# Layer 0's latents by feature blocks, weights stationary, from a transposed input

## Chip, cores and metric

One core of one Trainium2 chip. The metric is the device time of one execution of the whole program in microseconds (us), as the median of the runs shown. The program has two layers; the change lies in the first stage of layer 0.

## The reference, cut to what matters

SEQ = 2048 latent tokens and 256 context tokens run through two layers of width 1024. Layer 0 first modulates its input and projects it; the first 1056 columns are the latents of the attention heads:

```python
m = silu(cond) @ ada_w + ada_b                 # shift, scale, gate; one vector for x, one for the context
h = rms_norm(x, norm_g) * (1 + scale) + shift  # 2304 tokens x 1024
u = h @ w_in                                   # of it here: q_lat 768, kv_lat 256, k_rope 32
q  = (rms_norm(q_lat, q_norm) @ w_uq).reshape(n, 8, 96)
kv = (rms_norm(kv_lat, kv_norm) @ w_ukv).reshape(n, 8, 64 + 64)
k  = concat([kv[..., :64], broadcast(k_rope)])
q, k = rms_norm(q, q_gain), rms_norm(k, k_gain)
# the last 32 columns of q and k of the latent tokens are rotated (axial rope); v = kv[..., 64:]
```

The remaining columns of `u`, the attention itself, gated linear attention and layer 1 follow; they are not touched.

## The kernel before

Everything is f32. A large product is made of three products of rounded parts (`mm3`, lines 120 to 122: high by high, high by low, low by high), with each operand split into a high part `h` and a low part `l` by a pass of ScalarE (ACT) and one of VectorE (DVE). The three products are the only large work of TensorE (PE) in this stage.

`even_latent` works tile by tile: 18 tiles of 128 tokens (`NT`), the first two of them context. `prep` of a tile loads it as rows (`x`), sums its squares, scales it, turns it by eight transposes on PE (line 339, tile `px`), applies the modulation on ACT, splits it into `hhi` and `hlo`, and stores it to the scratch tensor `H`, from which later stages `reload` it. `gemm` then makes 3 x 8 x 3 products per tile with the token tile as the stationary side and 352 columns of `w_lat` (`W0`, `W1`, `W2`) as the moving side, so that a token's latents lie along a row (`u`). `scaled` takes the two root mean squares along that row and scales it. One step later `up` turns the tile again, eight transposes on PE (line 500, tile `tp`), splits it (`lth`, `ltl`), and makes the products with `w_uq` (`WU`, 36 of 384 columns) and `w_ukv` (`wkv`, 12 of 512 columns), followed by the norms and the rotation. One step later still `fin` turns q and k per head (16 transposes, line 554), splits four heads at a time into `qkhl` (two buffers) and stores them by DMAs on SP to `QA`, `QC`, `KA`, `KC`, in pieces of 512 bytes. So three tiles are in work at a time, and one tile's products stand among another's transposes and norms.

Beside that, `ada_first` makes the first modulation vectors from 8 MB of weights at the very start, and `ada_steps` makes the other eight rows of modulation in small steps: 64 loads `adaw` of 256 KB through two buffers, two DVE passes (`adac`) each, two products per row. `first` makes some of the next stage's products for the last two tiles, whose parts are kept, and `ahead` splits the next stage's weights (`w_rest`).

The order on each engine is laid down at build time: the framework places the recorded instructions by a timeline of its own and `issue_after` holds some back. Each engine, and SP and ACT as issuers of DMAs, then goes through its list in order. A DMA on SP or ACT takes one of eight semaphores in turn and waits until the DMA that had it before has landed.

`even_rest` follows: the remaining columns of `u`, woven with products (`mx`, line 660) for the maxima of the attention scores. These read `KA`, `KC`, `QA`, `QC` of all tiles back (`mk`, `mq`).

Of the kernel before, what the change touches and what calls it, by code (L numbers as in the profile page):

```python
# [88 lines left out]
class Kern:  # L89
# [151 lines left out]
    def ada_first(self, sp, pp, tags):  # L241
# [9 lines left out]
        for n, b in enumerate((0, 2, 1, 3)):  # L251
            ps = self.tl(pp, [P, 512], tags[0], bufs=2)
            for hf in range(2):
                w = self.tl(sp, [P, 4, 512], "adaw", bufs=8)
# [6 lines left out]
            pt = self.tl(pp, [P, 512], tags[1], bufs=2)  # L261
# [12 lines left out]
    def ada_steps(self, jobs, sp, pp, tag):  # L274

        nc = self.nc
        for l, b in jobs:
            acc = [self.tl(sp, [P, 512], f"adac{c}", bufs=1) for c in range(2)]
            for k in range(KD):
                w = self.tl(sp, [P, 512], "adaw", bufs=2)  # L280
# [120 lines left out]
    def even_latent(self, ws, wrest, kept):  # L401
# [6 lines left out]
        with ExitStack() as es:  # L408
            pp = self.pool(es, "epA", bufs=2, space=PSUM, reuse_waits="tile")
            px = ("px", 2)  # L410
            hT, lat, nat, win = {}, {}, {}, {}
            with ExitStack() as es2:
                st = self.pool(es2, "adaS", side="left", reuse_waits="tile")
                rows = self.transposed(0, self.i["xin"], pp, px, st)
                self.ada_first(st, pp, ("gm", "up"))
                hT[0] = self.modulate(0, 0, *rows)
                hi, lo = win[0] = [self.tl(ws, [P, KD, LAT_CHUNK], "W0" + z, F32R, bufs=1) for z in "hl"]
                for k in range(0, KD, 4):
                    w = self.tl(st, [P, 4, 512], "adaw", bufs=8)
                    nc.sync.dma_start(w[:, :, :LAT_CHUNK], self.i["w_lat"][:, 0, k : k + 4])  # L420
                    for n in range(0, 4, 2):
                        q = slice(k + n, k + n + 2)
                        self.act(hi[:, q, :], w[:, n : n + 2, :LAT_CHUNK])
                        nc.vector.tensor_tensor(out=lo[:, q, :], in0=w[:, n : n + 2, :LAT_CHUNK], in1=hi[:, q, :], op=ALU.subtract)
            wp = self.pool(es, "ewA", side="left", reuse_waits="tile")
            sp = self.pool(es, "esA", bufs=2, side="left", reuse_waits="tile")
            hT[1] = self.prep(0, 1, self.i["xin"], pp, px)
            for j in (1, 2):
                win[j] = self.split_w(ws, self.i["w_lat"][:, j], KD, LAT_CHUNK, f"W{j}", 2)
            behind = self.wload  # L430
            vec = self.tl(wp, [P, 8], "lnorm")
            nc.sync.dma_start(vec[:], self.i["lat_norm"])
            qkg = self.tl(wp, [P, 4], "qkg")
# [3 lines left out]
            wuq = self.split_w(ws, self.i["w_uq"], 6, 768, "WU", 1, rows=vec[:, 0:6])  # L437
            wkv = self.split_w(wp, self.i["w_ukv"], 2, 1024, "wkv", 1, rows=vec[:, 6:8])
# [4 lines left out]

            def gemm(*ts):
                us = {}
                for j in range(3):
                    for t in ts:
                        hi, lo = hT[t]
                        ps = self.tl(pp, [P, LAT_CHUNK], "gm", bufs=2)
                        wh, wl = win[j]  # L450
                        self.mm3(ps[:], (lambda k: hi[:, k, :], lambda k: lo[:, k, :]),
                                 (lambda k: wh[:, k, :], lambda k: wl[:, k, :]), range(KD))
                        if j == 0:
                            us[t] = self.tl(sp, [P, LAT_COLS], "u", bufs=2)
                        self.act(us[t][:, j * LAT_CHUNK : (j + 1) * LAT_CHUNK], ps[:])
                for t in ts:
                    parts = hT.pop(t)
                    if t >= NT - self.hbufs:
                        kept[t] = parts
                    scaled(t, us[t])  # L460

            def scaled(t, u):
                ss = self.tl(sp, [P, 4], "ssl")
                sq = self.tl(sp, [P, 512], "sql", bufs=1)
                self.act(sq[:, :512], u[:, :512], AF.Square, accum_out=ss[:, 0:1])
                self.act(sq[:, :256], u[:, 512:768], AF.Square, accum_out=ss[:, 3:4])
                nc.gpsimd.tensor_tensor(out=ss[:, 0:1], in0=ss[:, 0:1], in1=ss[:, 3:4], op=ALU.add)
                self.act(sq[:, :256], u[:, 768:1024], AF.Square, accum_out=ss[:, 1:2])
                self.act(sq[:, :32], u[:, 1024:], AF.Square, accum_out=ss[:, 2:3])
                self.rpow(ss[:, 0:1], ss[:, 0:1], 1.0 / Q_LORA, EPS)  # L470
                self.rpow(ss[:, 1:2], ss[:, 1:2], 1.0 / KV_LORA, EPS)
                nc.vector.tensor_scalar(out=u[:, :768], in0=u[:, :768], scalar1=ss[:, 0:1], scalar2=None, op0=ALU.mult)
# [105 lines left out]
            for s in range(NT + 2):  # L578
# [1362 lines left out]
```

## Time and profile before

| | us |
|---|---|
| runs | 3565.96, 3571.14, 3572.35 (median 3571.14) |
| profiled execution | 3570.04 |
| its span, first to last instruction | 3568.3 |
| PE busy | 3472.6 (97%) |
| DVE, ACT, POOL busy | 2341.2, 1389.5, 1275.0 |
| latent products on PE, first one | 35.17 |
| first product `mx` of the next stage | 564.88 |
| 0 to 570: PE busy, mean granted clock, DMA share | 527.92, 0.96, 0.60 |

How to read the rows quoted below: a row of a stretch has its length and then the busy time of PE, PE's weight loads, DVE, ACT and POOL with the number of instructions, PE's granted clock as a share of full speed, the DMA engines' mean busy share and GB/s. A row of the timeline has its start, its time, the engine, the line of the kernel, the operation, output and inputs, the shapes, and in brackets how long the engine stood idle before it and what ended that. A row of the chain of waits has a start, a time and what the chain passed through. A row of a group ends in its busy time, the mean of one in ns, and the idle time before it.

### The profile page before, as it was taken

The numbers are of one execution on the slowest core, as the hardware profiler recorded it, in microseconds if no ns is written. First come the engines' busy times: TensorE is split into PE (matmuls) and PEld (weight loads), VectorE is DVE, ScalarE is ACT, GpSimd is POOL, SyncE is SP. The second block draws the span as 40 slices with busy tenths as digits, with TensorE's granted clock in tenths as the row PEclk, the third lists the DMA queues.
The fourth block names the chain that finished last, engine by engine and source line by source line (L and its number), as shares of the span: only waits on it lengthen the run. The fifth ranks groups of instructions, "written<-read, shape, count | busy, mean of one in ns | idle before, by whom it ended". The sixth has DMA issues, their size and how long they took to land.

```text
span 3568.3 us, 53989 instructions
## 1 busy us (share of the span) xinstructions
PE 3472.6 (97%) x19604; PEld 2686.9 (75%) x19604; DVE 2341.2 (66%) x4624; ACT 1389.5 (39%) x2516; POOL 1275.0 (36%) x1411
## 2 busy tenths in 40 slices
PE   8999998999999999999999999999899999999899
PEld 6888987888896666665557878888688887555577
DVE  4677655888885777768874345455588784666732
ACT  5454552111113544546663124444322223555510
POOL 1333430100101333322212234333344443888763
PEclk9999999999999999999999999999999999999999
DMA  7555554222215242434526544445744447888672
GB/s 254 149 154 165 143 146 137 71 86 76 87 51 153 72 131 71 121 106 141 161 88 193 166 146 136 136 144 168 227 152 125 142 122 200 227 213 223 187 230 95
DMA packets 375868, 517.07 MB, mean 145 GB/s; under 512 B 34009, under 2 KB 253609, under 8 KB 369698
## 3 DMA queue, kind: packets, MB, share of 16 engines
q1 hardware_dynamic: 330914, 422.62, 41.3%
q0 software_dynamic: 22032, 63.00, 5.8%
q10 hardware_dynamic: 22656, 27.99, 2.2%
q8 instruction: 156, 2.56, 0.3%
q14 instruction: 110, 0.90, 0.1%
HBM read 334.17 MB, written 179.30 MB: 144 GB/s over the span
## 4 chain that ended last, share of the span: by engine, by line
PE 82%; DMA 6%; DVE 5%; ACT 2%; POOL 2%; issue 2%; SPq 1%; DVEq 0%; ACTq 0%; POOLq 0%
PE gm L129 10%; PE gm L130 10%; PE gm L131 10%; PE st L1130 9%; PE av L1040 7%; PE mx L660 4%; PE st L1587 2%; PE o L1621 2%; DMA wraw<-w_od 2%; PE pj L130 2%; PE pj L129 2%; PE pj L131 2%; PE st L131 2%; PE st L129 2%; PE st L130 2%
## 5 line engine op out<-in xcount | busy, mean ns | idle before, releaser
L661 DVE TENSOR_REDUCE mm<-mx 128x1 f32<-128x512 f32 (+1 forms) x656 | 388.4, 627 | 82.4 <-PE mx L660 75.3
L106 ACT ACTIVATE apt<-st 128x1024 f32<-128x1024 f32 (+1 forms) x296 | 300.3, 1015 | 304.9 <-PE st L1130 290.4
L1137 DVE TENSOR_TENSOR acc<-acc,apt 128x1024 f32<-128x1024 f32 x256 | 340.8, 1331 | 79.8 <-ACT apt L106 60.9
L1130 PE MATMUL st<-aq,akh 64*128 64x512 f32 x1728 | 312.0, 408 | 1.2 <-ACT apt L106 0.8
L1040 PE MATMUL av<-apt,av 128*64 128x512 f32 x1152 | 265.8, 598 | 0.0
L660 PE MATMUL mx<-mk,mq 96*128 96x512 f32 (+1 forms) x656 | 235.9, 373 | 1.0 <-DMA mq<-QC 0.6
L1746 DVE TENSOR_TENSOR opt<-st,tab 128x64 f32<-128x64 f32 (+10 forms) x576 | 144.2, 314 | 140.1 <-PE st L1588 63.9
L1627 POOL TENSOR_TENSOR oacc<-oacc,opt 128x576 f32<-128x576 f32 (+5 forms) x192 | 221.8, 1178 | 39.2 <-ACT rl L106 19.6
L1130 PE MATMUL st<-aq,akl 64*128 64x512 f32 (+1 forms) x1152 | 230.5, 390 | 0.0
L1130 PEld LDWEIGHTS st<-aq,akh 64*128 64x128 f32 x1728 | 152.8, 185 | 82.6 <-ACT apt L106 29.4
L106 ACT ACTIVATE u<-gm 128x352 f32<-128x352 f32 (+1 forms) x140 | 68.5, 497 | 368.3 <-PE gm L131 208.5
L1504 DVE CUSTOM_DVE_ANT_1 mx<-mx,mtab 128x217 f32<-128x217 f32 (+12 forms) x576 | 184.1, 338 | 39.9 <-PE mx L1498 30.6
L1040 PEld LDWEIGHTS av<-apt,av 128*64 128x64 f32 x1152 | 76.3, 136 | 135.2 <-issue 134.3
L106 ACT ACTIVATE opt<-opt 128x930 f32<-128x930 f32 (+8 forms) x130 | 104.3, 805 | 109.7 <-DVE opt L1746 106.4
L660 PEld LDWEIGHTS mx<-mk,mq 96*128 96x128 f32 x656 | 121.2, 188 | 13.7 <-DVE mm L661 1.6
L1130 PEld LDWEIGHTS st<-aq,akl 64*128 64x128 f32 (+1 forms) x1152 | 112.1, 184 | 22.9
L106 ACT ACTIVATE x<-px,modB,modA 128x128 f32<-128x128 f32 x272 | 99.5, 468 | 61.4 <-PE px L339 50.1
L129 PE MATMUL gm<-w1h,hhi 128*128 128x512 f32 x288 | 116.1, 403 | 7.3 <-ACT onat L106 7.3
L129 PE MATMUL gm<-w0h,hhi 128*128 128x512 f32 x288 | 115.3, 400 | 2.1 <-DVE hhi L351 2.1
L130 PE MATMUL gm<-w1l,hhi 128*128 128x512 f32 x288 | 114.7, 398 | 0.0
L210 POOL TENSOR_TENSOR oss<-oss,mhalf 128x8 f32<-128x8 f32 x68 | 112.4, 1653 | 5.1
L131 PE MATMUL gm<-w1h,hlo 128*128 128x512 f32 x288 | 113.9, 396 | 0.0
(506 smaller groups left out, 9716.9 us busy)
## 6 DMA issues: line engine op xcount, KB each, us to landing
q<-Q SPq DMA_DIRECT2D x48, 512.0 KB
H<-x ACTq DMA_DIRECT2D x36, 512.0 KB
adaw<-ada_w SPq DMA_DIRECT2D x64, 256.0 KB
x<-H SPq DMA_DIRECT2D x32, 512.0 KB
wraw<-w_od SPq DMA_DIRECT2D x64, 256.0 KB
K1t<-okt POOLq DMA_DIRECT2D x32, 512.0 KB, 7.7
kt<-K1t SPq DMA_DIRECT2D x32, 512.0 KB
mtab<-rpb_q SPq DMA_DIRECT2D x16, 899.0 KB
```

The lines of the kernel that those rows point to most:

```text
L106: return self.nc.scalar.activation(out, in_, func, **kw)
L129: self.nc.tensor.matmul(out, lh(k), rh(k), start=start and j == 0, stop=False)
L130: self.nc.tensor.matmul(out, lh(k), rl(k), start=False, stop=False)
L131: yield self.nc.tensor.matmul(out, ll(k), rh(k), start=False, stop=stop and j == n - 1)
L660: mm = nc.tensor.matmul(ps[:, :w], q[:A_QK, (t % 6) * P : (t % 6) * P + P], k[:A_QK, k0 : k0 + w], start=True, stop=True)
L661: nc.vector.tensor_reduce(out=m[:, t, n : n + 1], in_=ps[:, :w], axis=AX.X, op=ALU.max)
L1040: mm = nc.tensor.matmul(O[j, nb][i * 64 : i * 64 + 64, :w], V[j, kt // TT][:, kt % TT, i * 64 : i * 64 + 64], pts[:, i, :w], start=n == 0, ...
L1130: mm = nc.tensor.matmul(ps[:, o // 64, :w], k[o : o + r, kb, kq], Q[o : o + r, qb, :w], start=m == 0, stop=m == 4)
L1137: added = nc.vector.tensor_tensor(out=acc[:, :, :w], in0=a[:, :, :w], in1=pts[:, :, :w], op=ALU.add)
L1504: nc.vector.tensor_tensor_reduce(out=s, in0=s, in1=tb[:, ri : ri + rn, ci : ci + cn], scale=1.0, scalar=-3e38, op0=ALU.add, op1=ALU.max, a ...
L1627: self.psum = nc.gpsimd.tensor_tensor(out=a, in0=a, in1=pts[:, :, a0 - r0 : a1 - r0, :], op=ALU.add)
L1746: bias = nc.vector.tensor_tensor(out=pt[:, d[0], d[1]], in0=ps[:, d[0], d[1]], in1=tabs[j][i][:, ri : ri + rn, ci : ci + cn], op=ALU.add)
```

## The change

The input is also laid out transposed (`xT`, features on the partitions). `even_latent` now goes through six blocks of 256 or 512 tokens. Per block it takes the sums of squares with a product of ones (`stats`), applies norm and modulation in place, splits, and stores `H` by DMAs on ACT. The weights are the stationary side, eight feature blocks of 128 columns (`T0` to `T7`, all kept in SBUF); up to 512 tokens move. Each product's output has features on the partitions already; it is split (`lev`) and written to a scratch tensor `LT`, the high part on ACT's queue, the low part on SP's. The 32 rope columns are plain f32 products in four column groups. The sums of squares of the latents and the rope columns are brought back to token rows by small products (`rows`). When all blocks are done, `even_up` opens its own pools, splits `w_uq` and `w_ukv`, and goes through the 18 tiles: read the two parts from `LT`, `up` without transposes and with the scale applied in the eviction, `fin` two tiles later. The kept parts of the last two tiles are now reloaded from `H`. `w_lat` is laid out by feature block, and `ada_steps` uses the buffers `wraw`.

```diff
+    BLOCKS0 = [(0, CTX), (CTX, 256), (512, 512), (1024, 512), (1536, 512), (2048, 256)]
+    def even_latent(self, keep):
...
+            def stats(b, sp):
+                w = self.BLOCKS0[b][1]
+                acc = self.tl(sp, [P, w], "acc", bufs=1)
+                self.act(acc[:, :w], x[b][:, 0, :w], AF.Square)
+                for k in range(1, KD):
+                    sq = self.tl(sp, [P, w], "sq", bufs=3)
+                    self.act(sq[:, :w], x[b][:, k, :w], AF.Square)
...
+                ps = bank("st", 1)
+                nc.tensor.matmul(ps[:, :w], ones[:], acc[:, :w], start=True, stop=True)
...
+                    self.act(t[:, :w], ps[:, :w], AF.Ln)
+                    self.act(r[:, :w], t[:, :w], AF.Exp, scale=-0.5)
...
+            def modulate(b, r):
...
+                        nc.vector.tensor_tensor(out=v, in0=v, in1=r[:, :w], op=ALU.mult)
+                        self.act(v, v, AF.Identity, scale=self.modA[0][:, k, c : c + 1], bias=self.modB[0][:, k, c : c + 1])
+                        self.act(hi[:, n, :w], v)
+                        nc.vector.tensor_tensor(out=lo[:, n, :w], in0=v, in1=hi[:, n, :w], op=ALU.subtract)
...
+                for n in range(w // P):
+                    nc.scalar.dma_start(self.H[0, q0 // P + n].rearrange("p (k c) -> p k c", k=KD), xb[:, :, n * P : n * P + P])
...
+            def block(b, sp, ms):
+                w = self.BLOCKS0[b][1]
+                ps = [bank("gm", 4) for _ in ms]
+                for h in range(2):
+                    for p, m in zip(ps, ms):
+                        for n in range(4):
+                            for i, (a, v) in enumerate(terms(*W[m], hT[b][h])):
+                                nc.tensor.matmul(p[:, :w], a[:, h * 4 + n, :], v[:, n, :w],
+                                                 start=(h, n, i) == (0, 0, 0), stop=(h, n, i) == (1, 3, 2))
+                for p, m in zip(ps, ms):
+                    evict(b, sp, m, p)
+            def evict(b, sp, m, p):
...
+                hi, lo = [self.tl(sp, [P, 512], "lev", F32R, bufs=4) for _ in range(2)]
+                self.act(hi[:, :w], p[:, :w])
+                self.act(s[:, :w], p[:, :w], AF.Square)
+                nc.vector.tensor_tensor(out=lo[:, :w], in0=p[:, :w], in1=hi[:, :w], op=ALU.subtract)
...
+                for part, (v, q) in enumerate(((hi, nc.scalar), (lo, nc.sync))):
+                    q.dma_start(self.LT[part, t, :, m, :].rearrange("t p c -> p t c"), v[:, :w].rearrange("p (t c) -> p t c", c=P).bitcast(F32))
+            def rope_keys(b, sp):
...
+                        nc.tensor.matmul(ps[n * 32 : n * 32 + 32, :w], wr[:, h * 4 + n, :], xb[:, h * 4 + n, :w], start=h == 0, stop=h == 1)
...
+            for b in range(nb):
+                if b == 0:
+                    groups = [(m,) for m in range(M)]
+                else:
+                    groups = [(m, m + 1) for m in range(0, M, 2)]
+                for n, ms in enumerate(groups):
+                    block(b, sp, ms)
+                    if b and n == 0:
+                        if b + 2 < nb:
+                            load(b + 2)
+                        if b + 1 < nb:
+                            r = stats(b + 1, sp)
+                            modulate(b + 1, r)
+                            rope_keys(b + 1, sp)
+                    if b:
+                        with self.tc.issue_after(self.xload.ins):
+                            next(ada, None)
+                rows(b, sp)
...
+    def even_up(self, ws, kr, rs, wrest, kept):
...
+            wuq = self.split_w(ws, self.i["w_uq"], 6, 768, "WU", 1, rows=vec[:, 0:6])
+            wkv = self.split_w(wp, self.i["w_ukv"], 2, 1024, "wkv", 1, rows=vec[:, 6:8])
+            def fetch(t):
+                if t < NT:
+                    lat[t] = [self.tl(sp, [P, 8, P], "lt" + z, F32R) for z in "hl"]
+                    for part, v in enumerate(lat[t]):
+                        nc.sync.dma_start(v[:].bitcast(F32), self.LT[part, t])
...
-                for g in range(2):
-                    ps = self.tl(pp, [P, 4, P], "tp")
-                    for j in range(4):
-                        k = g * 4 + j
-                        nc.tensor.transpose(ps[:, j, :], u[:, k * P : k * P + P], self.ident[:])
...
-                    self.act(qn[:, h2 * 4 : h2 * 4 + 4, :], ps[:])
+                    self.act(qn[:, h2 * 4 : h2 * 4 + 4, :], ps[:], AF.Copy, scale=ss[0])
...
-                if s == 0:
-                    gemm(0, 1)
-                elif 1 < s < NT:
-                    gemm(s)
...
+                if s < NT:
+                    up(s)
+                    fetch(s + 2)
+                if s >= NT:
+                    first(NT - 1, s - NT + 2)
+                    first(NT - 2, s - NT + 2)
+                if 0 <= s - 2:
+                    fin(s - 2)
+                if s > 3:
+                    next(ahead, None)
+                if s in (NT - 3, NT - 2):
+                    t = 2 * NT - 4 - s
+                    kept[t] = self.reload(0, t)
...
+            keep = self.pool(e0, "kr", side="left", reuse_waits="tile")
+            parts = self.even_latent(keep)
...
-            self.even_latent(ws, win, hT)
+            self.even_up(ws, *parts, win, hT)
```

More of the change, by code (lines that the diff above doesn't have):

```diff
@@ L408, in even_latent @@
         with ExitStack() as es:
[L409 to L424, printed above, removed]
+            pp = self.pool(es, "epU", bufs=2, space=PSUM, reuse_waits="tile")
             wp = self.pool(es, "ewA", side="left", reuse_waits="tile")
             sp = self.pool(es, "esA", bufs=2, side="left", reuse_waits="tile")
[L427 to L430, printed above, removed]
+            lat, nat = {}, {}
             vec = self.tl(wp, [P, 8], "lnorm")
             nc.sync.dma_start(vec[:], self.i["lat_norm"])
+            wuq = self.split_w(ws, self.i["w_uq"], 6, 768, "WU", 1, rows=vec[:, 0:6])
[5 more added lines that the diff above has]
+                        nc.sync.dma_start(v[:].bitcast(F32), self.LT[part, t])
+            fetch(0)
+            fetch(1)
             qkg = self.tl(wp, [P, 4], "qkg")
@@ L442, in even_latent @@
             nc.sync.dma_start(sn[:], self.i["rope_sin"])
[L444 to L472, printed above, removed]
-                nc.vector.tensor_scalar(out=u[:, 768:1024], in0=u[:, 768:1024], scalar1=ss[:, 1:2], scalar2=None, op0=ALU.mult)
-                lat[t] = (u, ss)
             def rope(out, src, z, t, heads):
```

181 lines of the change are left out of this document (141 added, 40 removed).

## The prediction

> **What bounds the kernel now.** I read the page's busy shares first, then busy time by stretch, then the timeline at both ends of layer 0's latent stage.
>
> ```profile
> PE 3472.6 (97%) x19604; PEld 2686.9 (75%) x19604; DVE 2341.2 (66%) x4624; ACT 1389.5 (39%) x2516; POOL 1275.0 (36%) x1411
> 60.00:100.00 40.00, 32.50 (x166) 29.66 (x166) 29.50 (x47) 22.13 (x52) 11.59 (x18) 0.83 0.58 179
> 100.00:500.00 400.00, 393.61 (x2378) 363.35 (x2377) 279.42 (x528) 209.76 (x505) 157.50 (x297) 1.00 0.56 151
> 510.00:570.00 60.00, 45.15 (x226) 40.70 (x224) 26.67 (x48) 20.19 (x31) 10.11 (x11) 0.86 0.75 201
> 35.17 0.94 PE L120 MATMUL gm<-W0h,hhi 128*128 128x352 f32 x2
> 564.88 0.36 PE L660 MATMUL mx<-mk,mq 96*128 96x256 f32 x1 [0.57 <-DMA mq<-QC]
> ```
>
> TensorE (PE, the first column of a stretch) is the bound: 97% of the span, 393.6 of 400 us in the middle of the stage, at a full granted clock (third number from the end). At the ends it isn't: 60 to 100 us waits for weights at clock 0.83, 510 to 570 us runs the last tiles' chains at 0.86. The DMA engines (second to last) are 0.56 busy in the middle. The stage's first product stands at 35.2 us; the next stage's first key-maximum product, which needs every tile's Q and K written, at 564.9. I call that second point M. In the two built programs the instructions from shortly after M on stand in the same order on PE, VectorE (DVE) and ScalarE (ACT), so the change is worth the shift of M. The sum is against the profiled execution, 3570.0 us, of which 3568.3 are the span; the median of the runs, 3571.1, is 0.03% above it.
>
> **Prices on PE.** Products overlap, so the price is the distance between starts:
>
> ```profile
> 407.59 0.32 PE L120 MATMUL gm<-W2h,hhi 128*128 128x352 f32 x1
> 407.75 0.32 PE L121 MATMUL gm<-W2l,hhi 128*128 128x352 f32 x1
> 409.24 0.39 PE L120 MATMUL up<-wkvh,lth 128*128 128x512 f32 x1
> 409.48 0.39 PE L121 MATMUL up<-wkvl,lth 128*128 128x512 f32 x1
> 521.63 0.34 PE L120 MATMUL up<-WUh,lth 128*128 128x384 f32 x1
> 521.81 0.34 PE L121 MATMUL up<-WUl,lth 128*128 128x384 f32 x1
> 565.77 0.28 PE L660 MATMUL mx<-mk,mq 96*128 96x256 f32 x1
> 565.89 0.39 PE L129 MATMUL gm<-WUh,hhi 128*128 128x512 f32 x1
> 113.85 0.87 PE px L339 x8
> 119.40 1.81 PE tp L291 x4
> 22.18 1.05 PE L264 MATMUL up<-adasel,adarow 128*128 128x2 f32 x8
> ```
>
> So 352 columns cost 0.16 us, 512 cost 0.234, 384 cost 0.177, 256 cost 0.12: about 0.46 ns a column everywhere. A wider moving side buys nothing by itself. A 128-column transpose costs 0.11. A plain f32 product of 512 columns leaves two records, so the four are two products of 0.9 us; the narrow ones of 2 columns cost 1.05/4 = 0.26.
>
> Removed: 1296 latent products of 352 columns (207 us), 144 input transposes and 144 latent transposes (31 us). Added: 576 products of 256 and 576 of 512 columns (69 + 135 = 204 us); 54 narrow row products (14 us); six f32 column sums (4 us); 48 f32 products for the rope columns. For those I have bounds only: alone, 24 of 0.9 and 24 of 0.45 make 32 us; four column groups side by side would make 8. The built order puts a few next to each other and most between other products, so I take 20. Result: 238 us out, 242 in. **PE's work does not shrink.** What decides is how much of it finds no cover. In the old loop a tile's latent products, 72 x 0.16 = 11.5 us, lie between its neighbours' up-projection and transposes and hide their chains; the new second stage has only up-projection and transposes.
>
> **First stage, latents by blocks.** The start needs a first x block of 1 MB, 8.4 MB of modulation weights, another 1 MB of x and 1 MB of w_lat.
>
> ```profile
> DMA packets 973, 6.77 MB, mean 423 GB/s; under 512 B 109, under 2 KB 109, under 8 KB 184
> GB/s 279 410 328 66 98 16 0 0 0 0 0 0 0 0 0 0 0 0 0 0 0 0 0 111 180 188 193 184 180 193 184 154 322 232 156 199 158 268 201 35
> QA<-qkhl SPq DMA_DIRECT2D x4, 128.0 KB
> QC<-qkhl SPq DMA_DIRECT2D x2, 128.0 KB
> ```
>
> The first row is the DMA view of 10 to 26 us, with pieces of 2 KB and more: 423 GB/s. The strip is 100 to 110 us in 40 slices, where QA and QC are written in 512-byte pieces: a plateau of 180 to 193, say 185. At 423, 11.4 MB take 27 us from 2.6 us on, plus some 4 us for splitting the first weight: the first product at 34 us against 35.2.
>
> PE then has 242 + 16 us (the later modulation rows, 16 products of 0.9 and their transposes, which come along) = 258 us. The DMA engines have LT (2 x 9.4 MB written in 512-byte pieces, 102 us), H (9.4 MB, now also in 512-byte pieces, 51 us) and 39 MB of x and weights at 423 (92 us): 245 us, under PE's 292 but four fifths busy. ACT and DVE per block of 512:
>
> ```profile
> L106 ACT ACTIVATE lth<-tp 128x512 fp32r<-128x512 f32 x36 | 21.2, 600 | 29.3 <-PE tp L500 29.3
> L352 DVE TENSOR_TENSOR hlo<-x,hhi 128x512 fp32r<-128x512 f32 x36 | 24.7, 685 | 0.4
> L286 DVE SCALAR_TENSOR_TENSOR adac<-adaw,condT,adac 128x512 f32<-128x512 f32 x112 | 79.4, 745 | 16.1 <-DMA adaw<-ada_w 15.4
> 0.73 1.28 ACT L106 ACT_TABLE_LOAD   x1 [0.73 <-PEq L1932]
> 397.53 12.00 SPq L281 DMA_DIRECT2D adaw<-ada_w  x6
> ```
>
> ACT: 43 passes of 0.6 and two table loads, 28 us, plus 12 DMA issues. DVE: 24 passes of 0.685, three of the statistic, 32 of 0.745 for modulation, 43 us. PE: 45 + 10. So PE bounds a full block, DVE following closely. Not so the blocks of 256: their PE time is 23 to 28 us, but in the first ACT also splits eight weights, and in the second all 32 modulation passes stand ahead of the next block's scaling on DVE. Their 16 loads come at 12/6 = 2 us apiece at best, 32 us. Behind a DVE that waits for such a load stand the evictions' low parts; behind those the LT writes on SP. At the second block's end I expect 8 us of idle PE, 5 elsewhere (bounds 0 and 30). The stage ends at 34 + 258 + 13 = 305.
>
> **The seam.** ACT's order has the last evictions, then a reloaded H tile, then the splits of WU. On SP four LT loads (2.1 MB) and H (0.5 MB) stand ahead of the third w_uq slice.
>
> ```profile
> 52.18 3.22 DMA wraw<-w_uq
> 55.42 0.95 ACT WUh L106
> 56.39 1.03 DVE WUl L396
> 57.44 3.23 DMA wraw<-w_uq
> ```
>
> These are two raw buffers in turn: 5.3 us a round. Evictions 1.5; the loads ahead 8.5 (2.6 MB at 423 are 6.2, and a slice of 0.39 MB took 3.2 where 423 gives 0.9, so 2.3 is latency); the reload's split 1, the first pair 3, two more rounds 10.5: about 25 us to the whole WU; w_ukv one round more, 30; then the first tile's products, twelve products that wait for w_rest, the second tile's queries at 36 x 0.177 = 6.4: 42 us to the first Q/K split. PE works some 15 us of it (bounds for the seam 30 and 46). Before, the same weights came at 60 to 100 us, at the price of PE's 7.5 idle us and the low clock there; that goes.
>
> **Second stage.** Its beat is the Q/K split qkhl, 18 tiles x 4 = 72 of them through two buffers, each written by three DMAs.
>
> ```profile
> 527.10 0.69 ACT L106 ACTIVATE qkhl<-tp,qkg 96x512 fp32r<-96x512 f32 x1
> 529.83 0.68 ACT L106 ACTIVATE qkhl<-tp,qkg 96x512 fp32r<-96x512 f32 x1 [0.53 <-DVE vn L521]
> 532.28 0.69 ACT L106 ACTIVATE qkhl<-tp,qkg 96x512 fp32r<-96x512 f32 x1 [0.83 <-DMA QC<-qkhl]
> 529.38 0.61 SPq L563 DMA_DIRECT2D QC<-qkhl  x1
> 511.09 4.36 DMA QC<-qkhl
> 550.10 1.40 ACT L106 ACTIVATE qkhl<-tp,qkg 96x512 fp32r<-96x512 f32 x2
> ```
>
> At the old stage's end, with little else in flight, splits follow each other every 2.6 us and the last waits for the DMA issued at 529.38; behind such a wait stand, in ACT's order, the next tile's evictions, and behind those PE. Three floors per split: PE (36 x 0.177 + 12 x 0.234 + 16 x 0.11 = 10.9 us a tile) 2.7; the DMA engines (1.57 MB at 185 and 1.3 MB of LT and Vn at 423 = 11.6 us a tile) 2.9; the buffer cycle 2.6, or 3.4 where a QC write takes 4.36 us rather than those 2.9 (6.7 us for two). I take 3.0, just above the floor by the DMA engines: 216 us. From the last split to M, 564.9 - (550.1 + 0.7) = 14.
>
> Sum: 305 + 42 + 216 + 14 - 3 (the last beat is in both) = 574, against 565. **Forecast 3570 + 9, rounded to 3580 us.** A measurement of this kernel tells 0.2%, some 7 us, from no change.
>
> **Rivals.** *Faster: the second stage is PE's.* If 512-byte writes cost less than the plateau says, the beat is 2.7 (196 us); with no idle in the first stage and a seam of 36: 34 + 258 + 36 + 196 + 11 = 535, 3540 us. For it: the mean DMA share of 0.56 leaves room in the old stage. Against it: the plateau, and the wait on QC with an idle neighbourhood. 22%. Here the Trainium skill, "DMA: Bandwidth & Descriptors" (Specifications), says that transfers from 512 bytes up run at line rate. By that rule 2.9 MB a tile would take 6.8 us and this rival would hold; the strip speaks against it.
>
> *Slower still: modulation loads starve DVE.* If the 2 us per load become 4 beside LT and H writes, the four blocks with 16 loads each take 64 us or more: 64 + 3 x 64 against 28 + 8 + 3 x 55 is 55 more, partly hidden; with half of it and a beat of 3.4 (29 us more), M is at 631 and the time 3636 us. It decides once a load takes over 55/16 = 3.4 us. For: 16 us of DVE waits on adaw in its row, with far fewer writes in flight. 10%.
>
> *No change:* the beat is 2.9 and the seam 40: M within 7 us of 565. 16%. That the change doesn't do what it says is out: the built program holds 1152 + 48 + 6 + 54 products in place of 1584.
>
> **Numbers.** The forecast case has 52%; slower in all 62%, same 16%, faster 22%. From the bounds, M = (34 + 246) + 30 + 196 + 11 = 517 at best and (34 + 270 + 30) + 46 + 245 + 11 = 636 at worst (rope columns 8 or 32, beat 2.7 or 3.4), 3522 to 3641; both ends need every term at its bound, so the range is 3538 to 3620.
>
> **What would show it.** Right: the first M product at 570 to 580; the last latent product near 305; a gap on PE of over 15 us behind it with WU and w_uq as releasers; a second stage with PE about nine tenths busy, DMA share over 0.85, ACT's qkhl waiting for QC or KC. Wrong: PE at 98% there (the beat is PE's), or a first stage past 325 with DVE waiting for adaw, or a shift behind M, where I expect none.

## The result, and the profile after

The changed kernel takes 3668.23 us (median of four runs, 3664.74 to 3676.09) against 3570.15 for the kernel before beside it: a ratio of 1.0273, 95% interval 1.0251 to 1.0296. It is slower, as forecast, by 98 us where the forecast had 9; 3668 lies outside the range of 3538 to 3620.

The profiled execution took 3664.7 us, of which the span is 3662.9; before, 3570.0 and 3568.3. First the page's busy shares, then busy time by stretch (columns as before), in the stretches that the marks below give:

```profile
PE 3514.9 (96%) x19388; PEld 2654.4 (72%) x19388; DVE 2374.6 (65%) x4649; ACT 1387.6 (38%) x2371; POOL 1305.7 (36%) x1382
```

```profile
37.00:345.00 308.00, 282.37 (x1390) 203.12 (x1390) 205.03 (x313) 129.33 (x247) 87.35 (x81) 0.93 0.59 174
345.00:395.00 50.00, 30.49 (x126) 25.56 (x127) 19.27 (x25) 17.77 (x24) 14.46 (x30) 0.69 0.69 227
395.00:643.00 248.00, 211.44 (x1155) 186.16 (x1154) 159.89 (x314) 112.63 (x188) 102.53 (x177) 0.94 0.77 219
643.00:654.00 11.00, 7.84 (x44) 6.84 (x42) 3.31 (x5) 2.41 (x4) 0.77 (x1) 1.00 0.94 228
37.00:654.00 617.00, 532.14 (x2710) 421.68 (x2710) 387.49 (x657) 262.13 (x460) 205.11 (x289) 0.92 0.68 197
```

The same row of the kernel before, from its first latent product to M:

```profile
35.00:565.00 530.00, 499.71 (x2931) 461.24 (x2930) 353.72 (x645) 270.99 (x624) 179.94 (x326) 0.96 0.58 160
```

The marks come from the timeline by tile; a row has the number of instructions, minimum, median and maximum in ns, and the first and last start:

```profile
L487 PE MATMUL gm<-hhi,T0h x8: 278/284/468, 37.0 to 42.2; 128*128 128x256 f32 x8
L487 PE MATMUL gm<-hhi,T7l x16: 278/336/497, 302.1 to 344.3; 128*128 128x512 f32 x8, 128*128 128x256 f32 x8
L122 PE MATMUL up<-WUh,lth x2: 522/605/688, 359.2 to 359.7; 128*128 128x384 f32 x2
L108 ACT ACTIVATE qkhl<-tp,qkg x72: 666/683/687, 395.1 to 642.5; 96x512 fp32r<-96x512 f32 x72
L799 PE MATMUL mx<-mk,mq x10: 282/396/628, 654.0 to 664.7; 96*128 96x512 f32 x7, 96*128 96x256 f32 x3
```

The first latent product starts at 37.0, the last at 344.3, the first up product at 359.2; the 72 Q/K splits go from 395.1 to 642.5; M is at 654.0 where it was 564.9. So 89.1 of the span's 94.6 us lie ahead of M and 5.5 behind it. Between the first latent product and M the row of 617 us has 532.1 busy, 84.9 idle; that of 530 us had 499.7 and 30.3. Two us later start, 55 more idle, 32 more busy at a lower clock (0.92 against 0.96) make the 89.

Each term of the forecast has its mark:

| us | forecast | measured | difference |
|---|---|---|---|
| first latent product | 34 | 37.0 | +3 |
| first stage, to the last latent product | 271 | 307.3 | +36 |
| seam, to the first Q/K split | 42 | 50.8 | +9 |
| second stage, first to last split | 213 | 247.4 | +34 |
| last split to M | 14 | 11.5 | -2 |

(The forecast's 216 for the second stage counted one beat twice and took it off at the end; 213 is without it.)

**The first stage, read in the chain at its second block.** The waits of 37 to 345 us, each with its total, count and longest:

```profile
PE gm L487 <- DVE lev L502: 8.4, 2, 5.7
PE st L438 <- DVE acc L435: 8.1, 2, 4.9
ACT L108 <- PE st L438: 35.3, 4, 14.5
DVE adac L286 <- DMA wraw<-ada_w: 19.4, 2, 14.0
```

and how they hang together, in the timeline of 84 to 101 us (rows between left out):

```profile
84.17 7.98 POOL L433 TENSOR_TENSOR acc<-acc,sq 128x512 f32<-128x512 f32 x5
...
93.74 0.75 DVE L288 SCALAR_TENSOR_TENSOR adac<-wraw,condT,adac 128x512 f32<-128x512 f32 x1 [1.30 <-DMA wraw<-ada_w]
...
95.40 0.67 DVE L435 SCALAR_TENSOR_TENSOR acc<-sq,acc 128x512 f32<-128x512 f32 x1
...
96.13 2.08 PE L438 MATMUL st<-acc,ones 128*128 128x512 f32 x2 [3.18 <-DVE acc L435]
98.28 1.28 ACT L108 ACT_TABLE_LOAD   x1 [8.82 <-PE st L438]
...
100.07 0.38 ACT L108 ACTIVATE sq<-gm 128x256 f32<-128x256 f32 x1
...
100.48 0.42 DVE L502 TENSOR_TENSOR lev<-gm,lev 128x256 fp32r<-128x256 f32 x1 [0.44 <-ACT sq L108]
...
100.96 0.58 PE L487 MATMUL gm<-hhi,T6h 128*128 128x256 f32 x1 [2.76 <-DVE lev L502]
```

GpSimd's additions of the next block's squares end only at 92.15; one modulation load is late, and the last addition, on DVE, stands behind that pass and two more until 95.40; the column sum (`st`) waits for it on PE, with all latent products behind it; the table load waits 8.82 us for the column sum on ACT, with two finished evictions (`sq`, `lev`) behind it; and the next latent product waits for a PSUM bank that these evictions hold. No engine is full here (DVE comes nearest, with 30.9 of the 35 us from 85 to 120): lists in fixed order wait for each other.

**The second stage.** What ACT's splits waited for, from their timeline:

```profile
  DMA QC<-qkhl: 54.2, 21
  DMA KC<-qkhl: 26.2, 19
```

That is 80 us in 40 waits for the write that frees one of the two `qkhl` buffers, while the DMA engines are 0.77 busy.

### The profile page after: what moved, and what is told of

Read it like the earlier page. It is cut to its first block, busy times and chain, and to the rows that moved or that the text cites. A ratio compares the mean times of both kernels' runs of the same rounds, so it can differ in the third digit from the quotient of the medians.

```text
span 3662.9 us, 53768 instructions
## 1 busy us (share of the span) xinstructions
PE 3514.9 (96%) x19388; PEld 2654.4 (72%) x19388; DVE 2374.6 (65%) x4649; ACT 1387.6 (38%) x2371; POOL 1305.7 (36%) x1382
## 5 line engine op out<-in xcount | busy, mean ns | idle before, releaser
L1766 POOL TENSOR_TENSOR oacc<-oacc,opt 128x576 f32<-128x576 f32 (+5 forms) x192 | 222.8, 1183 | 36.8 <-ACT rl L108 16.6
L108 ACT ACTIVATE u<-gm 128x352 f32<-128x352 f32 (+1 forms) x86 | 44.4, 517 | 334.2 <-PE gm L133 216.4
L133 PE MATMUL gm<-w0h,hlo 128*128 128x512 f32 x288 | 114.0, 396 | 0.0
```

The lines of the kernel that those rows point to most:

```text
L108: return self.nc.scalar.activation(out, in_, func, **kw)
L133: yield self.nc.tensor.matmul(out, ll(k), rh(k), start=False, stop=stop and j == n - 1)
L1766: self.psum = nc.gpsimd.tensor_tensor(out=a, in0=a, in1=pts[:, :, a0 - r0 : a1 - r0, :], op=ALU.add)
```

## Experiments

All single marks below come from one profiled execution of each kernel; the whole time is the median of four runs for the changed kernel, e8 and e10, and one run for the others. e1, e2 and e11 leave work out, as their texts say. The four kernels with the same first stage (changed, e3, e4, e12) take 305.7 to 310.2 us for it, and what lies behind M takes 3007.9 to 3022.6 us, so the marks are compared rather than whole times, and differences under some 5 us are left alone.

| kernel | first latent | last latent | first up | first split | last split | M | whole time |
|---|---|---|---|---|---|---|---|
| changed | 37.0 | 344.3 | 359.2 | 395.1 | 642.5 | 654.0 | 3668.2 |
| e1 | 37.5 | 315.2 | 330.8 | 368.7 | 617.8 | 629.3 | 3643.3 |
| e2 | 38.7 | 334.0 | 349.0 | 385.1 | 630.9 | 643.0 | 3667.8 |
| e3 | 38.2 | 348.4 | 361.3 | 386.1 | 644.0 | 655.8 | 3669.8 |
| e4 | 37.8 | 345.0 | 358.0 | 382.4 | 611.6 | 625.4 | 3643.7 |
| e5 | 38.7 | 349.7 | 363.0 | 387.1 | 611.7 | 625.4 | 3639.2 |
| e6 | 37.3 | 326.2 | 339.1 | 363.5 | 593.4 | 607.4 | 3626.7 |
| e7 | 37.0 | 310.8 | 323.8 | 348.3 | 579.2 | 594.0 | 3610.4 |
| e8 | 36.8 | 313.1 | 327.1 | 349.7 | 572.6 | 589.1 | 3600.3 |
| e9 | 38.3 | 337.9 | 350.5 | 374.8 | 604.2 | 618.5 | 3634.9 |
| e10 | 37.1 | 313.3 | 319.1 | 346.4 | 573.3 | 587.8 | 3602.7 |
| e11 | 37.5 | 299.7 | 315.4 | 342.2 | 600.1 | 611.8 | 3627.2 |
| e12 | 36.1 | 341.8 | 350.1 | 380.2 | 602.5 | 618.1 | 3627.8 |

**e1: without the interleaved modulation passes.**

```diff
-            for k in range(KD):
+            for k in range(1):
                 w = self.tl(sp, [P, 512], "wraw", bufs=2)
```

> Left out: seven of the eight weight slices of each interleaved modulation row, their loads and both of their accumulating passes (so the gates and layer 1's modulations are wrong; 98 of the 112 interleaved accumulating passes of 0.94 us and 112 of 128 loads go). Marks in the changed kernel: last latent product starts at 344.3, first Q/K split at 395.1, first product of the next stage at 653.9. Theory A (the first stage is late because VectorE stands behind those passes and their late loads, so PSUM banks, the statistics and then TensorE wait): PE's idle time between 37 and 345 falls from 27 to under 10, the last latent product comes at 312 to 325, the later marks shift by as much. Rival B (the stage is late because its TensorE work is heavier than summed: rope products, clock): the last latent product stays at 335 or later.

The first stage takes 277.7 us in place of 307.3, M comes 24.7 sooner, and PE's idle time nearly goes. Its busy time by stretch:

```profile
37.00:316.00 279.00, 275.42 (x1391) 200.10 (x1390) 113.19 (x202) 130.16 (x248) 78.71 (x82) 0.98 0.47 140
```

Theory A holds for 30 of the 36 us. But 277.7 with 4 idle is also more than the 258 that the forecast took for PE's work, so part of B holds too.

**e2: without GpSimd's additions.**

```diff
-                    if k < KD - 1:
-                        g.tensor_tensor(out=acc[:, :w], in0=acc[:, :w], in1=sq[:, :w], op=ALU.add)
-                    else:
+                    if k == KD - 1:
...
-                if m != first:
-                    g.tensor_tensor(out=a[:, :w], in0=a[:, :w], in1=s[:, :w], op=ALU.add)
```

> Left out: GpSimd's additions of squares in the first stage, both those of the input's statistics (of eight squares the last one and the first are kept) and those of the latents' (only one square each), so scales are wrong. Theory A (the additions, 1.1 to 1.6 us each, hold back ScalarE's squares and so the statistics product, the table loads and everything queued on ScalarE behind them, and they slow VectorE's accumulating passes, 936 ns against 745 ns before): the accumulating pass falls below 800 ns, ScalarE's wait for the statistics product from 35 to under 15, and the last latent product from 344 to 325-335. Rival B (ScalarE's waits for the statistics have another cause, VectorE's queue): the last latent product within 4 us of 344; the pass keeps its 936 ns if the slowing isn't GpSimd's.

The group of modulation passes, first in the changed kernel, then here (before: 745 ns in the prediction's row):

```profile
L288 DVE SCALAR_TENSOR_TENSOR adac<-wraw,condT,adac 128x512 f32<-128x512 f32 x112 | 100.6, 936 | 16.2 <-DMA wraw<-ada_w 16.0
```

```profile
L288 DVE SCALAR_TENSOR_TENSOR adac<-wraw,condT,adac 128x512 f32<-128x512 f32 x112 | 79.7, 746 | 40.6 <-DMA wraw<-ada_w 40.4
```

GpSimd's additions stretch VectorE's passes by a quarter; without them a pass is back at 746 ns. The Trainium skill, "SBUF — State Buffer" (SBUF: two separate sides), says that the two engines share a pair of ports, which a VectorE instruction with two inputs in SBUF and a GpSimd instruction hold exclusively in turn; the two rows agree with it. The stage shortens by 12 us (295.3), and ACT's wait for the column sum falls from 35.3 to 24.3 us only, not under 15: the additions are one cause, not the main one. Time saved on DVE turned largely into waits for the loads, 16.0 to 40.4 us. Behind M this execution lost what it had won before it; that is why the whole time doesn't show it.

**e3, e4, e12: the seam's order, and a third buffer for the split.** e3 holds the two reloads back (`with tc.issue_after(...)` around `self.reload(0, t)`); e4 adds a third buffer to that; e12 moves one small load on top of e4.

```diff
-        x = self.tl(sp, [P, D], "x", bufs=1)
+        x = self.tl(sp, [P, D], "wraw" if l == 0 else "x", bufs=self.wbufs if l == 0 else 1)
...
-                        hl = self.tl(sp, [P, 4, 2, P], "qkhl", F32R, bufs=2)
+                        hl = self.tl(sp, [P, 4, 2, P], "qkhl", F32R, bufs=3)
```

> The two reloads of modulated tiles are held until late in the up stage, so that ScalarE's first weight split does not queue behind a reloaded tile. Theory A (the seam is ScalarE's order: its split of a reloaded tile waited 12 us for a transfer while w_uq was there): the first up product comes 7 to 9 us after where it was relative to the last latent product (14.9 us after it now, 6 to 8 then), the first Q/K split 6 to 9 us sooner, the first product of the next stage as much. Rival B (the five rounds of load then split of the weights carry the seam whatever comes first): first Q/K split at most 3 us sooner.

> The held reloads and three buffers instead of two for the split Q/K tile (the room comes from the reload's own tile, which now takes a slot of the raw weights). Theory A (the second stage's beat of 3.44 us, 72 in 247.4, is the cycle of two buffers: split, write, free): the beat falls to 2.9-3.1 and the stage from 247 to 210-222; ScalarE's waits for the QC and KC writes fall from 80 to under 25. Rival B (the transfers themselves are the limit, 512 bytes a piece): beat 3.3 or more, the same waits for the writes. Rival C (TensorE at a lowered clock): beat 3.3 or more with the waits gone.

> e4 with one load moved: the column of norm weights (4 KB), which the first weight split needs, is read in the first stage instead of behind the latents' reads on SP (in e4 ScalarE waited 11.0 us for it at the seam). Theory A: the seam of 37.4 us falls to 27-31, the second stage keeps 225-232, the first product of the next stage comes at 615 to 619 (625.4 in e4). Rival B: the second stage takes it back, TensorE being behind w_ukv, w_rest and the first tiles' chains: seam and stage together 263 or more (266.6 in e4).

e3's theory holds for one of its three marks. The first Q/K split comes 9.0 us sooner (37.7 us after the last latent product, 50.8 before), but the first up product still comes 12.9 us after the last latent one (14.9), and M stays (655.8). Most of what the first split gained is order, not time: in the changed kernel 72 up products of 384 columns, 18 of 512 and 20 products of `first` stand ahead of it, in e3 37, 12 and none (10.8 us less by the prediction's prices), and the second stage is 10.5 us longer. ACT's waits at the seam, in e3, say what held the first up product:

```profile
ACT WUh L108 <- DMA lnorm<-lat_norm: 11.0, 1, 11.0
```

The scale column of 4 KB, which the first weight split needs, stood on SP behind 2 MB of latents (and a reload, in the changed kernel). e12 reads it early: the first up product comes 8.3 us after the last latent one, M at 618.1, 7.3 sooner than in e4, of which 3.2 lie ahead of the last latent product. The expected seam of 27 to 31 us didn't come: the first split stands 38.4 us after the last latent product, with 16 more up products of 384 columns ahead of it than in e4, and what is gained shows in the second stage (222.3).

e4 is clear. The two kernels differ in the buffer (and in the place of the reloaded tile): the second stage falls from 257.9 in e3, 247.4 in the changed kernel, to 229.2 us, M from 655.8 to 625.4. ACT's splits then wait

```profile
  DMA QC<-qkhl: 11.5, 5
  DMA KC<-qkhl: 10.9, 4
```

and the stretch of the stage has

```profile
382.00:612.00 230.00, 213.52 (x1215) 195.41 (x1214) 161.44 (x322) 116.14 (x195) 105.23 (x180) 0.98 0.86 247
```

The DMA engines carry 247 GB/s where they carried 219, so they were not the limit; PE is busy 213.5 of 230 us. Two buffers were. The beat is 3.23 us, above the 2.9 to 3.1 expected: PE's own work alone is 213 us, 3.0 a beat, and not 196 (below).

**e5, e6, e9, e11: the rope products and the bursts.** e6 gives DVE the same passes in portions of two; e5 and e9 make the rope columns from the split halves.

```diff
                         nc.vector.scalar_tensor_tensor(out=a[:], in0=w[:], scalar=self.condT[:, k, c : c + 1], in1=a[:],
                                                        op0=ALU.mult, op1=ALU.add)
-            yield
+                yield
...
-                            next(ada, None)
+                            for _ in range(4):
+                                next(ada, None)
```

```diff
-                        nc.tensor.matmul(ps[n * 32 : n * 32 + 32, :w], wr[:, h * 4 + n, :], xb[:, h * 4 + n, :w], start=h == 0, stop=h == 1)
+                        for i, v in enumerate(hT[b][h]):
+                            nc.tensor.matmul(ps[:64, :w], wr[:, h * 4 + n, :], v[:, n, :w],
+                                             start=(h, n, i) == (0, 0, 0), stop=(h, n, i) == (1, 3, 1))
```

> Built on e4. The interleaved modulation rows are the same work and the same loads, but VectorE gets them in portions of two passes, four portions after each pair of latent chunks, where it got sixteen passes at once after every other pair. Theory A (it is the burst: sixteen passes of 0.94 us and their loads stand ahead of evictions, and four PSUM banks cover one pair only): the first stage shortens by 12 to 25 us of the 30 that leaving them out gave, PE's waits for evictions and statistics fall from 17 to under 6. Rival B (it is VectorE's whole load or the lateness of the loads): 5 us or less.

> Built on e4 (last latent product 345.0, first stage 307.2 from its first product, first product of the next stage 625.4). The rope columns' eight plain f32 products per block, in four column groups, become sixteen products of the split halves that the latents use already, with the rope weights' high and low parts side by side as 64 stationary columns. Theory A (the rope products are what made TensorE's work in the first stage larger than summed: 80 records, 31 us busy, against 16 x 0.22 x 4.5 = 16 us now): the first stage shortens by 11 to 17 us. Rival B (TensorE waits for VectorE anyway, so less work becomes idle time): 4 us or less, PE's idle time grows by the difference.

> e6 (portions) with e5's rope products alone, the squares as in the changed kernel. Theory A (a plain f32 rope product of 512 columns costs TensorE 0.97 us wherever it stands, 36 of them in 512-column equivalents against 96 products of 16.9 us in all, and e5 gained nothing only because bursts on VectorE set its stage): the first stage falls from e6's 288.9 to 268-275, with e7's 273.8 then owing nothing to the square sums. Rival B (the gain of e7 came from the square sums and their place): 282 or more.

> Built on e1 (no interleaved modulation passes; its first stage, 277.7 us, is TensorE's with some 5 us idle). Left out besides: seven of the eight rope products of each block (keys' rope columns wrong). Theory A (a plain f32 rope product of 512 columns costs 0.97 to 1.0 us though it fills 32 of 128 columns, 36 of them in 512-column equivalents make 35 to 39 us, where the prediction took 20): the stage falls by 29 to 35 us to 243-249. Rival B (20 was about right and the surplus is the lowered clock and issue): it falls by 14 to 20, to 258-264.

e6: 288.9 us where e4 has 307.2, 18 of the 30 that leaving the passes out gave, with the same passes at 933 ns (919 in e4) and the same loads. PE's waits for evictions and statistics fall from 17 to 8.2 us, not under 6. It is the burst. Its price is paid in the order of the lists, not in DVE's load.

e5 and e9 did the opposite of what I expected. PE's rope work falls (start to start from 27.9 to 18.1 us in e5, from 26.3 to 17.0 in e9), and the stage gets longer: 311.0 against 307.2 in e4, and 299.6 against 288.9 in e6. PE's waits in e5, and then in e9:

```profile
PE tp L293 <- DVE adac L288: 13.9, 4, 7.1
PE rp L518 <- ACT hhi L108: 10.6, 5, 3.9
...
PE rp L518 <- DVE hlo L461: 4.6, 3, 3.2
```

```profile
PE tp L293 <- DVE adac L288: 9.9, 4, 7.5
PE rp L518 <- ACT hhi L108: 6.9, 4, 3.8
```

The plain f32 product needs only the modulated `x`; the new ones need the split halves, the last step of the chain, and PE now waits for them more (at the rope products 4.6 us in e4, 0.3 in e6). The modulation rows' products, too, wait longer for their passes (3.1 us in e4, 2.1 in e6). Why these moved, and how the loss divides between the two, is not shown.

e11 leaves seven of eight rope products out on top of e1: 262.2 us against 277.7, so 15.5, inside B's band and below A's. The forecast's 20 for all of them was nearly right as a net effect. One product by itself is dearer than that, as the timeline of the changed kernel shows (a plain f32 product leaves two records):

```profile
176.84 0.39 PE L487 MATMUL gm<-hlo,T6h 128*128 128x512 f32 x1
177.15 1.05 PE L516 MATMUL rp<-x,Tr 128*32 128x512 f32 x2
178.13 0.49 PE L487 MATMUL gm<-hhi,T6l 128*128 128x512 f32 x1
```

From 176.84 to 178.13 are 1.29 us, of which a latent product among its like takes 0.234: the rope product costs 1.06 (0.98 to the next start, and 0.08 that the latent product ahead of it takes longer). Where two rope products stand side by side, in different column groups, both together take the same 0.98, to the next product at 187.48:

```profile
186.50 1.05 PE L516 MATMUL rp<-x,Tr 128*32 128x512 f32 x4
```

So the prediction's lower bound, four groups side by side, is borne out for two; the built order puts most of these products singly. Some of what leaving it out saves comes back as a lower granted clock (0.95 over e11's first stage, 0.98 over e1's).

**e7, e8, e10: the parts together.** e7 adds to e4 the portions, e5's rope products, now behind the last pair of chunks, and square sums by TensorE, without GpSimd, with the squares a block ahead. e8 also loads and splits `w_uq` and reads the norm column early; e10 puts the first latents ahead of `w_ukv` on SP.

```diff
+                more = b and b + 1 < nb
+                if more:
+                    squares(b + 1)
                 for n, ms in enumerate(groups):
                     block(b, sp, ms)
+                    if more and n == 0:
+                        mean(b + 1)
+                    if more and n == 1:
+                        r = root(b + 1, sp)
+                        modulate(b + 1, r)
+                    if more and n == 3:
+                        rope_keys(b + 1, sp)
```

```diff
+                            if (b, n) == (nb - 2, 2):
+                                ra = self.tl(hp, [P, KD, 512], "x", bufs=2)[:].rearrange("p a b -> p (a b)")
+                                nc.sync.dma_start(ra[:, : 5 * 768].rearrange("p (k c) -> p k c", k=5), self.i["w_uq"][:, :5])
...
```

> Built on e4, with e5's rope products, e6's portions, and the input's square sums made by TensorE (eight f32r products per block, no additions on GpSimd, the squares a block ahead in the tiles of the low halves), logarithm and root behind the second pair's evictions, the rope products behind the last pair. Theory A (the first stage is then TensorE's alone: 204 us of latent products, 16 of rope, 8 of square sums, 16 of modulation rows, 14 of row products, and 5 to 10 idle): the stage takes 258 to 270 us where e4's took 307. Rival B (ScalarE or the DMA engines are next): 280 or more, with PE idle over 25 us.

> e7, and at the seam the up-projection's query weights are loaded into free input and product tiles during the last two blocks and split as soon as the latents' weights leave, the norm column is loaded in the first stage. Theory A (the seam is loads in line, two raw buffers at a time, and a norm column behind 2 MB of latents): the first Q/K split comes 18 to 26 us after the last latent product (e4: 37), the second stage keeps its 225 to 232 us, being TensorE's; the first product of the next stage stands at 545 to 562 where the kernel before has 564.9, the time 3548 to 3568. Rival B (the second stage takes back what the seam gives, as in e3, where 13 us of seam became 10 us of stage): seam and stage together 260 or more, first product of the next stage 565 to 580, time 3568 to 3590.

> e8 with the first latent tile's two reads ahead of the key and value weights' loads on SP (in e8 the first up product waited 10.9 us for the latents behind a load that waited for a weight split). Theory A (the rest of the seam is that order): the first up product comes 4 to 7 us after the last latent product (14.0 in e8), the first product of the next stage at 577 to 582, the time 3586 to 3592. Rival B (what the seam gives the second stage takes back): it stays at 586 or later. In neither case is the kernel before (564.9) reached: TensorE's own 270 + 219 us plus the start at 37 and an end of 14 to 16 make 540 to 542, and two fillings and one draining of the chain lie on top.

e7's first stage is 273.8 us, 4 above its band, and of PE's waits (26 us in the changed kernel) these are left:

```profile
PE rp L524 <- DVE hlo L467: 3.3, 2, 2.6
PE tp L293 <- DVE adac L288: 2.9, 1, 2.9
PE gm L493 <- DVE lev L508: 0.3, 1, 0.3
```

The rope products of e5 and e9, now behind the last pair, wait 3.3 us for their operands. e9's theory, that the cheaper product alone explains e7, fell with e9; so e7's gain over e6 (15 us) comes from the new places and the square sums, which were not separated.

e8 and e10 gave little: M at 589.1, outside both of e8's bands, and at 587.8 (e7 594.0); 3600.3 and 3602.7 us, ratios to the kernel before of 1.0082 (1.0065 to 1.0099) and 1.0083 (1.0066 to 1.0100). In both, seam and second stage together take 260 us, B's figure: e10's seam is 3.5 us shorter than e8's and its second stage 4.0 longer. Of the 98 us 68 are recovered; no version beats the kernel before. What is left can be read in e8's row from the first latent product to M:

```profile
37.00:589.00 552.00, 507.69 (x2742) 433.27 (x2742) 367.08 (x650) 259.87 (x465) 174.67 (x264) 0.95 0.76 222
```

Against the row of the kernel before: 2 us later start, 8 more busy, 44.3 idle in place of 30.3. Nearly half of that idle time lies in two stretches, the seam, which the old loop didn't have, and the end:

```profile
313.00:350.00 37.00, 22.98 (x115) 21.00 (x114) 18.42 (x26) 17.23 (x25) 15.23 (x30) 0.82 0.60 209
573.00:589.00 16.00, 9.93 (x40) 8.40 (x40) 4.25 (x6) 3.82 (x6) 1.34 (x2) 0.79 1.00 274
```

## Why the prediction was wrong

**The direction and the reason were right.** "PE's work does not shrink", and what decides is how much of it finds no cover: that is what the rows say. A wider moving side bought nothing: 256 columns took 0.12 us, 512 took 0.234, start to start, as priced. The shift of M is the change, but for 5.5 of 95 us. The sign alone says little: the 9 us forecast lay just above the 7 that a measurement tells from no change.

**The step that failed first: "258 us" and "13", the first stage's work and idle time, +36 us.** Taking, for every product, the distance to the next start, the 307.3 us divide into latents 234.8 (13.3 of them idle), rope 27.6, modulation rows 20.0 (3.8 idle), column sums 13.3 (8.4 idle), token rows 10.5 and transposes 1.3. That makes 25.5 idle where 13 were taken, inside the bounds of 0 and 30. But the products themselves took 282 and not 258, and these had no bounds except for the rope columns: rope 27.6 in place of 20, latents 221.5 in place of 204. In e1, with hardly a gap, the latents still take 217.4. Some 8 of its 13 surplus us lie in products of 512 columns next to a plain f32 product (0.33 to 0.35 us on average in place of 0.234), the rest mostly in products of 256 columns at about 0.2 in place of 0.12: half of these next to plain f32 products too, half at a granted clock of 0.50 (38 to 42 and 97 to 100 us). I took prices from runs of like products and summed them as if the kinds didn't meet.

The gaps come on top, with the clock that follows them:

```profile
85.00:120.00 35.00, 20.79 (x85) 11.28 (x83) 30.89 (x42) 17.20 (x31) 10.96 (x10) 0.71 0.38 108
```

Their mechanism was in part the slower rival's ("modulation loads starve DVE"), which I gave 10% and tied to a load time of 3.4 us. It didn't need that: the burst of sixteen passes, which I saw ("all 32 modulation passes stand ahead of the next block's scaling on DVE") and priced at 8 us at one block's end, came at later blocks as well (PE is busy 5.1 of the 10 us from 150 and 4.3 of those from 230), with the pass at 936 ns in place of the 745 that I carried over from a kernel in which GpSimd had no squares to add. The sign named for it, a first stage past 325 with DVE waiting for its loads, came (344; 19.4 us at L286 and 16.0 at L288). What I did not see is the chain on ACT, table load behind column sum with evictions behind both.

**The second step: the beat of the second stage, 3.48 us in place of 3.0 (+34).** Two errors. The bound by PE left out the products of `first` that stand in this stage: 95 of 352 columns, 17.0 us start to start in the changed kernel, 115 and 21.2 in e4. With them PE's work between the first and the last split was 211 us in the changed kernel and 213 in e4, 3.0 a beat and not 2.7, although the up products of one to two of the 18 tiles stand ahead of the first split. So the forecast's 213 us had PE almost without idle time. And of the three floors I took the DMA engines' as the one that binds; it was the buffer cycle, whose 3.4 from a QC write of 4.36 us stood in the text as the upper bound. e4 shows it: one more buffer, 28.7 us less than e3, with more bytes per second. The faster rival's condition, 512-byte pieces cheap enough for the DMA engines to keep up, was thus half true. They kept up at 247 GB/s, which doesn't make its time: PE's floor was higher and the buffers came first. The rule of the Trainium skill quoted with it ("DMA: Bandwidth & Descriptors", Specifications), line rate from 512 bytes on, isn't borne out: in the kernel before, from 105.75 to 107.75 us, with such writes alone, the engines moved 177 GB/s at a DMA share of 0.91, and in e8's last stretch, a mix with larger pieces, 274 at 1.00, against 423 in loads without pieces of 512 bytes.

**The third: the seam, 50.8 in place of 42 (+9).** Above the upper bound of 46. The sum had all of `w_ukv` split 30 us after the last latent product. It was 35.2 us in the changed kernel, 32.5 in e3 without the reloads, 30.2 in e12 with the column read early besides, as the ends of these rows show (changed kernel, e3, e12; single executions, so the steps of 2 to 3 us are rough):

```profile
378.33 1.15 ACT L108 ACTIVATE wkvh<-wraw,lnorm 128x1024 fp32r<-128x1024 f32 x1
379.72 1.15 ACT L108 ACTIVATE wkvh<-wraw,lnorm 128x1024 fp32r<-128x1024 f32 x1 [0.58 <-DMA wraw<-w_ukv]
370.83 1.15 ACT L108 ACTIVATE wkvh<-wraw,lnorm 128x1024 fp32r<-128x1024 f32 x1
```

I had the 2.6 MB ahead of the third weight slice and one reload, but not the second reload between the slices, nor the 4 KB column that the first slice needs too (ACT waited 11.0 us for it in e3 and e4). Small operands of the first instruction belong in such a sum. Of the other 4 us, behind `w_ukv`, some 2.7 by the prediction's prices are 6 more products of 512 columns and 8 more of `first` ahead of the first split than the sum had; the rest stays open.

**Behind M** I expected nothing, and 5.5 us came. The variants have 3007.9 to 3022.6 us there with nearly the same lists, the changed kernel 3008.9, the kernel before 3003.4. The cause stays open.

All terms but the end erred to the same side. The worst case by bounds, M at 636 and so still below the measured 654, was left outside the range because both ends "need every term at its bound". The terms are not independent: in the first stage, at the seam and in the second stage alike, lists in fixed order wait with nothing beside them.

## What to carry to other kernels

When one woven loop is cut into two stages, count not only each engine's work but what used to stand between the steps of each chain: here the same work with less cover lost 55 us to idle time and ran at a lower clock besides. Sum every product in a stage before calling it a bound, and then ask of each buffer whether its whole round, down to the landed write, fits into the beat; one more buffer was worth 29 us of its stage here, and cutting a burst of sixteen passes into twos 18.

## What was unexpected of the hardware

A VectorE pass over two SBUF inputs took 936 ns on average beside GpSimd's additions and 746 without them. A plain f32 product with 32 stationary columns cost 1.06 us for 512 columns when it stood alone between other products, 0.08 of that in the latent product ahead of it; two of them side by side in different column groups took 0.98 to the next start, no longer than one.
